# Attention probabilities turned by VectorE blocks and DMA in place of TensorE transposes

## The chip, the cores and the metric

The kernel runs on one core of one Trainium2 chip. A core has a matrix engine (TensorE, PE in the profile), a vector engine (VectorE, DVE), a scalar engine (ScalarE, ACT), a general engine (GpSimd, POOL), a queue engine (SyncE, SP), and sixteen DMA engines that serve the queues of SP, ACT and POOL. PE multiplies a stationary operand, loaded by a separate instruction (PEld in the profile), with a moving one and writes into eight PSUM banks of 128 x 512 float32; DVE and ACT carry results from PSUM to SBUF. [...] Each engine runs its instructions in the order in which they were written out, and waits for other engines and transfers by semaphores.

The metric is the device time of one execution, in microseconds.

## The reference

Two layers over 512 tokens of width 1024 in float32: dilated attention and a gated feed-forward block, then an mLSTM mixer and a second feed-forward block, then a norm. The change touches the attention:

```python
def banded_window_attention(q, k, v, window):
    ...                                     # blocks of 128 queries, each with its own and the previous block of keys
    s = jnp.einsum('...iqd,...ikd->...iqk', qb, kk).astype(jnp.float32)
    s = jnp.where(valid, s, -jnp.inf)
    m = jnp.max(s, axis=-1, keepdims=True)
    p = jnp.exp(s - m)
    den = jnp.sum(p, axis=-1, keepdims=True)
    o = jnp.einsum('...iqk,...ikd->...iqd', (p / den).astype(v.dtype), vv)
    lse = (m + jnp.log(den))[..., 0]
    ...

def dilated_attention_mixer(xn, positions, w_in, w_out):
    proj = (xn @ w_in).reshape(B, S, N_GROUPS, 3, ATTN_HEADS, ATTN_HEAD_DIM)   # 1024 x 9216
    for g, (window, dilation) in enumerate(((128, 1), (512, 4), (2048, 16))):
        q = apply_partial_rope(proj[:, :, g, 0], positions) * scale
        k = apply_partial_rope(proj[:, :, g, 1], positions)
        o, lse = dilated_window_attention(q, k, proj[:, :, g, 2], window, dilation)
        ...
    wts = jax.nn.softmax(jnp.stack(lses), axis=0)
    o = jnp.einsum('gbsh,gbshd->bshd', wts, jnp.stack(outs))
    return o.reshape(B, S, ATTN_WIDTH) @ w_out
```

There are eight heads of 128. Per head the three groups give 15 blocks of 128 queries by 128 keys: seven for group 0 (four diagonal ones and three with the previous block) and four each for groups 1 and 2. The product with the values needs each of these blocks with the keys on the partitions, while the softmax needs them with the queries there: each block of probabilities has to be turned.

## The kernel before

**Projections.** Weights come from DRAM in chunks of 512 KB on SP's queue (`load_chunk`, L186). Each is split into a high and a low part, `_h` by ACT (L198) and `_l` by DVE (L199), with three buffers per part, and each product is three matmuls, high by high, low by high, high by low (`multiply`, L224). `project` (L234) computes 256 columns as two accumulators in two chunks; three PSUM banks (`acc`) hold accumulators. After each chunk it calls `advance()`, which moves a clock of ticks on by one. A tick is 24 matmuls of 512 columns, or 48 of 256 in the token form (`project_tokens`, L251).

**Order around the change.** Attention works on four pairs of heads (`attention_pair`, L451). Per pair there are nine projections, 18 ticks: q and k of groups 0, 1 and 2 (ticks 1 to 12), then v of groups 0, 1 and 2 (13 to 18). The attention work proper is put between the projections' matmuls by `defer(n, fn)`, which calls `fn` n ticks later, and `run` (L155), which keeps the PE instructions of the called functions together as one block: it is issued after the last PE instruction before it, and later projection matmuls are held behind its last one (`fenced`, L167). The places are lists of ticks:

- `scores0` at +2 after k of group 0; the others are counted from the end of the group 2 k projection (tick 12): `scores12` at +3, `weigh` with `turn` at +5, `transposes(0)` at +6, `values(0)` with `transposes(1)` at +7, `values(1)` at +8. The last pair has `LAST_AT`, one tick less from the weigh run on; +7, +8 and so on reach into the projections of the next pair, or, for the last, into the output projection.
- `scores0` (L463) and `scores12` (L486): scores on PE, mask and maximum on DVE, exponentials on ACT, into `p0` (seven blocks) and `p12` (eight blocks) of each head of the pair.
- `weigh` (L539): one PE matmul exchanges sums between token orders (L530), about ten small DVE instructions form the factors, and sixteen DVE instructions scale `p0` and `p12` in place (L560, L563), head 0 first.
- `turn` (L565): turns v of group 0 on PE, from `vf0` in a tag `vf` with one buffer.
- `transposes(i)` (L574): 15 PE transposes of head i's blocks into four PSUM banks (tags `s` and `o`, two each), each carried by ACT to SBUF (L582) into one of `PT_BUFS` = 4 buffers of 128 x 512.
- `values(i)` (L585): 15 matmuls accumulate the head's 128 x 512 output in one PSUM bank (tag `t`, one buffer), which ACT carries out to `o_heads` (L601). In the trace each shows as two records, 14 of line 594 and 16 of line 599.

After the fourth pair, `split_act` splits the finished heads (L213, L214), `last_heads` (L656) the last two; the output projection follows in four column parts of two chunks each, the first inside the attention's scope, with the last pair's late runs in it.

Of the kernel before, what the change touches and what calls it, by code (L numbers as in the profile page):

```python
# [11 lines left out]
F32 = mybir.dt.float32  # L12
# [19 lines left out]
C1 = 6.28125  # L32
C2 = float(np.float32(np.uint32(np.float32(TWO_PI - C1).view(np.uint32) & 0xFFFFF000).view(np.float32)))
C3 = float(np.float32(TWO_PI - C1 - C2))
PT_BUFS = 4
RUN_AT = (2, 3, 5, 6, 7, 8)
LAST_AT = (2, 4, 5, 6, 7)
STACK_AT = (9, 11, 14, 16)
HEAD_AT = ((9, 11, 13), (10, 13, 15), (12, 15, 17), (13, 16, 18), (15, 18, 19), (16, 19, 21), (18, 21, 22), (19, 21, 23))
W_BUFS = 3  # L40
# [30 lines left out]
def tile_hybrid_dilated_attn_mlstm(  # L71
# [8 lines left out]
    def pool(stack, name, **kw):  # L80
        return stack.enter_context(tc.tile_pool(name=name, bufs=1, **kw))
# [50 lines left out]
    def defer(n, fn):  # L132
        later.append((tick[0] + n, next(order), fn))
# [33 lines left out]
    def fenced():  # L167
        return tc.issue_after(fence[0]) if fence[0] is not None else nullcontext()

    def acc_tile(name):  # L170
        return ps.tile([P, 512], F32, tag="acc", name=name, bufs=3)
# [21 lines left out]
    def split_chunk(chunk):  # L193

        raw, n, view, name = chunk
        hi = wp.tile([P, 1024], F32R, tag="whi", name=name + "_h", bufs=W_BUFS)
        lo = wp.tile([P, 1024], F32R, tag="wlo", name=name + "_l", bufs=W_BUFS)
        nc.scalar.activation(hi[:, :n], raw[:, :n], AF.Copy)  # L198
        nc.vector.tensor_tensor(lo[:, :n], raw[:, :n], hi[:, :n].bitcast(F32), op=ALU.subtract)  # L199
        return view(hi), view(lo)  # L200
# [70 lines left out]
    def transpose_into(dst_ps, i, src, n=P):  # L271
        nc.tensor.transpose(dst_ps[:, i * n:(i + 1) * n], src, ident)  # L272
# [38 lines left out]

    with ExitStack() as actx:
        ap = pool(actx, "attn")

        first_w = []
        R = 32
# [32 lines left out]
                nc.gpsimd.tensor_copy(cosn[:, c * P:(c + 1) * P], cs[s])  # L349

        def tok_tile(name):
            return ap.tile([P, 2, SEQ], F32, tag="qk", name=name, bufs=8)


        xt = {}
# [69 lines left out]
        def by_block(t):  # L425

            return t.rearrange("p (c b j) -> p b c j", c=4, b=TB)
# [23 lines left out]
        def attention_pair(pr):  # L451
# [8 lines left out]
            def score_bank(i, name):  # L460
                return ps.tile([P, 512], F32, tag="so"[i], name=name, bufs=2)
# [24 lines left out]
            def scores12(qk1, qk2):  # L486

                for i in range(2):
                    p12[i] = ap.tile([P, 8, P], F32, tag="p12", name="%sp12_%d" % (nm, i), bufs=2)
                    for g, (q, k) in ((1, qk1), (2, qk2)):  # L490
                        sp = score_bank(i, "%ss%d" % (nm, g))
                        for c in range(4):
                            sl = slice(c * P, (c + 1) * P)
                            nc.tensor.matmul(sp[:, sl], q[:, i, sl], k[:, i, sl], start=True, stop=True)
                        for c in range(4):
                            sl = slice(c * P, (c + 1) * P)
                            nc.vector.tensor_tensor_reduce(
                                p12[i][:, 4 * (g - 1) + c, :], sp[:, sl], mask_causal if g == 1 else mask_dil,
                                1.0, -3e38, op0=ALU.add, op1=ALU.max, accum_out=mx[:, g - 1, i, c:c + 1])
                    exponentials(1, i)  # L500
# [71 lines left out]
                                             scale=rnat[:, b:b + 1])  # L572

            def transposes(i):  # L574
                pts[i] = []
                for b, (src, n0, n1) in enumerate(((p0[i], 0, 4), (p0[i], 4, 7), (p12[i], 0, 4), (p12[i], 4, 8))):
                    tp = score_bank(b // 2, nm + "pT")
                    for j in range(n0, n1):
                        transpose_into(tp, j - n0, src[:, j, :])
                    t = ap.tile([P, 512], F32, tag="pt", name=nm + "pTs", bufs=PT_BUFS)  # L580
                    w = (n1 - n0) * P
                    nc.scalar.activation(t[:, :w], tp[:, :w], AF.Copy)  # L582
                    pts[i].append(t)

            def values(i):  # L585
                pt = pts[i]
                hs = slice(i * P, (i + 1) * P)
                op = ps.tile([P, 512], F32, tag="t", name=nm + "o", bufs=1)
                first = True
                for b in range(4):  # L590
                    for kb in range(max(b - 1, 0), b + 1):
                        idx = 2 * b - (b - kb)
                        src = pt[idx // 4][:, (idx % 4) * P:(idx % 4 + 1) * P]
                        nc.tensor.matmul(by_block(op)[:, b], vt[0][:, kb, hs], src,
                                         start=first, stop=False, skip_group_check=True)
                        first = False
                for g in (1, 2):
                    for c in range(4):
                        nc.tensor.matmul(op[:, c * P:(c + 1) * P], vt[g][:, c, hs], pt[1 + g][:, c * P:(c + 1) * P],
                                         start=False, stop=(g == 2 and c == 3), skip_group_check=True)  # L600
                nc.scalar.activation(o_heads[2 * pr + i], op, AF.Copy)  # L601

            qks = []
            for g in range(3):
# [19 lines left out]
                if g == 0:  # L624
                    defer(RUN_AT[0], lambda: run(lambda: scores0(*qks[0])))
            later_runs = (
                (lambda: scores12(*qks[1:]),), (weigh, turn),
                (lambda: transposes(0),), (lambda: values(0), lambda: transposes(1)), (lambda: values(1),))
            for at, fns in zip(RUN_AT[1:] if pr < HEADS // 2 - 1 else LAST_AT, later_runs):
                defer(at, lambda fns=fns: run(*fns))  # L630
            for g in range(3):
                v = ap.tile([P, TB, 256], F32, tag="v", name="%sv%d" % (nm, g), bufs=4)
                vt.append(v)

                def evac_v(m, acc, v=v):
                    for i in range(2):
                        tb = 2 * m + i
                        nc.scalar.activation(v[:, tb, :], acc[:, i * 256:(i + 1) * 256], AF.Copy,
                                             scale=rtok[:, tb:tb + 1])
                if g == 0:  # L640

                    vf0, v0 = ap.tile([P, 2, SEQ], F32, tag="vf", name=nm + "vf"), v

                    def evac_f(m, acc, vf=vf0):
                        nc.scalar.activation(in_order(vf[:, m]), by_block(acc), AF.Copy)
                    project(pair, w_in, 2 * D + pr * 256, KC, evac_f, nm + "g0v")
                else:
                    project_tokens(pair, w_in, g * 3 * D + 2 * D + pr * 256, evac_v, "%sg%dv" % (nm, g))
# [16 lines left out]
        def out_project(pairs, w2d, nk, name, first=0, end=KC // 2):  # L665
            for c in range(first, end):
                project(pairs, w2d, c * 256, nk, add_to_h(c), "%s%d" % (name, c))


        defer(1, last_heads)  # L670
        out_project(pair, attn_w_out[0], KC, "awo", end=1)
        assert not later
    out_project(pair, attn_w_out[0], KC, "awo", first=1)


    def norm(key, k0, name):
# [454 lines left out]
```

## Time and profile before

| | |
|---|---|
| median of the runs | 1482.21 us (1481.99 to 1483.33, three runs) |
| profiled execution | 1481.93 us, span 1479.8 us |
| granted TensorE clock | 0.999 |
| DMA | 134.70 MB, 91 GB/s over the span; SP's queue 28.8% of sixteen engines' time, POOL's 0.1% |
| busy from 30 to 460 us (430 us) | PE 430.00, DVE 246.19, ACT 147.84, POOL 0.00 |

The pairs of attention fill the first 470 us or so. The page shows for each engine how long it was busy. Matmuls overlap, so their lengths add up to more than the time they take; the cost of one is the distance between the starts of two that follow each other. The names in a row are output <- inputs, with buffer numbers left out (`a1pT<-cst,a1p` writes the transposed probabilities of pair 1). The number behind an arrow in a row is the idle time before it and what ended that. A row of DMA issues gives the KB of one transfer and the median time from its issue to its landing.

### The profile page before, as it was taken

The numbers are of one execution on the slowest core, as the hardware profiler recorded it, in microseconds if no ns is written. First come the engines' busy times: TensorE is split into PE (matmuls) and PEld (weight loads), VectorE is DVE, ScalarE is ACT, GpSimd is POOL, SyncE is SP. The second block draws the span as 40 slices with busy tenths as digits, with TensorE's granted clock in tenths as the row PEclk, the third lists the DMA queues.
The fourth block names the chain that finished last, engine by engine and source line by source line (L and its number), as shares of the span: only waits on it lengthen the run. The fifth ranks groups of instructions, "written<-read, shape, count | busy, mean of one in ns | idle before, by whom it ended". The sixth has DMA issues, their size and how long they took to land. (4 is left out here: it accounts for less than half of the span.)

```text
span 1479.8 us, 18900 instructions
## 1 busy us (share of the span) xinstructions
PE 1463.7 (99%) x7484; PEld 1250.0 (84%) x7484; DVE 766.5 (52%) x1507; ACT 545.2 (37%) x997; POOL 102.7 (7%) x94
## 2 busy tenths in 40 slices
PE   7999999999999999999999999999999999999998
PEld 6899889889889888888888889798888888888887
DVE  7754654654665463343343338987755443343233
ACT  5333325225226342232232223785543333233223
POOL 1000000000000001111110000000000111110011
PEclk9999999999999999999999999999999999999999
DMA  6322222232232223333323233231233233322232
GB/s 191 100 86 72 86 86 72 86 96 76 63 99 81 72 87 102 97 100 100 99 84 103 93 94 87 58 100 58 80 106 97 90 98 100 100 92 94 85 100 72
DMA packets 127528, 134.70 MB, mean 91 GB/s; under 512 B 5392, under 2 KB 119376, under 8 KB 127440
## 3 DMA queue, kind: packets, MB, share of 16 engines
q1 hardware_dynamic: 125328, 131.55, 28.8%
q10 hardware_dynamic: 1808, 1.38, 0.3%
q8 instruction: 59, 0.97, 0.3%
q0 software_dynamic: 304, 0.56, 0.1%
q14 instruction: 29, 0.24, 0.0%
HBM read 131.38 MB, written 2.10 MB: 90 GB/s over the span
## 5 line engine op out<-in xcount | busy, mean ns | idle before, releaser
L229 PE MATMUL f0j<-n_h,f0j_h 128*128 128x512 f32 x352 | 137.1, 389 | 0.0
L229 PE MATMUL f1j<-n_h,f1j_h 128*128 128x512 f32 x352 | 137.1, 389 | 0.0
L229 PE MATMUL f0j<-n_h,f0j_l 128*128 128x512 f32 x352 | 137.0, 389 | 0.0
L229 PE MATMUL f1j<-n_h,f1j_l 128*128 128x512 f32 x352 | 137.0, 389 | 0.0
L229 PE MATMUL f0j<-n_l,f0j_h 128*128 128x512 f32 x352 | 136.9, 389 | 0.0
L229 PE MATMUL f1j<-n_l,f1j_h 128*128 128x512 f32 x352 | 136.9, 389 | 0.0
L199 DVE TENSOR_TENSOR f0j_l<-f0j_w,f0j_h 128x1024 fp32r<-128x1024 f32 x44 | 54.8, 1245 | 54.9 <-ACT f0j_h L198 54.8
L199 DVE TENSOR_TENSOR f1j_l<-f1j_w,f1j_h 128x1024 fp32r<-128x1024 f32 x44 | 54.8, 1246 | 54.6 <-ACT f1j_h L198 54.6
L229 PEld LDWEIGHTS f1j<-n_h,f1j_l 128*128 128x128 f32 x352 | 66.1, 188 | 13.9
L229 PEld LDWEIGHTS f0j<-n_h,f0j_l 128*128 128x128 f32 x352 | 66.1, 188 | 13.9
L229 PEld LDWEIGHTS f1j<-n_l,f1j_h 128*128 128x128 f32 x352 | 66.1, 188 | 13.8
L229 PEld LDWEIGHTS f0j<-n_h,f0j_h 128*128 128x128 f32 x352 | 66.1, 188 | 13.8
L229 PEld LDWEIGHTS f0j<-n_l,f0j_h 128*128 128x128 f32 x352 | 66.1, 188 | 13.5
L229 PEld LDWEIGHTS f1j<-n_h,f1j_h 128*128 128x128 f32 x352 | 66.1, 188 | 13.5
L198 ACT ACTIVATE f0j_h<-f0j_w 128x1024 fp32r<-128x1024 f32 x44 | 46.5, 1057 | 73.6 <-PE f0j L229 72.5
L198 ACT ACTIVATE f1j_h<-f1j_w 128x1024 fp32r<-128x1024 f32 x44 | 46.5, 1057 | 73.3 <-PE f1j L229 72.2
L1063 PE MATMUL fin<-fw_h,f1ah 128*128 128x512 f32 (+1 forms) x198 | 72.8, 368 | 0.0
L1063 PE MATMUL fin<-fw_l,f1ah 128*128 128x512 f32 (+1 forms) x198 | 72.5, 366 | 0.0
L1063 PE MATMUL fin<-fw_h,f1al 128*128 128x512 f32 (+1 forms) x198 | 72.4, 366 | 0.0
L229 PE MATMUL fo<-f0ah,fo_k_l 128*128 128x512 f32 x176 | 68.5, 389 | 0.0
L229 PE MATMUL fo<-f0al,fo_k_h 128*128 128x512 f32 x176 | 68.5, 389 | 0.0
L229 PE MATMUL fo<-f0ah,fo_k_h 128*128 128x512 f32 x176 | 68.5, 389 | 0.0
(1160 smaller groups left out, 3569.7 us busy)
## 6 DMA issues: line engine op xcount, KB each, us to landing
f0j_w<-in_ffn_w_in_dram SPq DMA_DIRECT2D x44, 512.0 KB, 3.6
f1j_w<-in_ffn_w_in_dram SPq DMA_DIRECT2D x44, 512.0 KB, 3.5
fw_w<-in_ffn_w_out_dram SPq DMA_DIRECT2D x22, 512.0 KB, 3.8
fo_k_w<-in_ffn_w_out_dram SPq DMA_DIRECT2D x20, 512.0 KB, 3.4
awo_k_w<-in_attn_w_out_dram SPq DMA_DIRECT2D x8, 512.0 KB, 3.5
mv_k_w<-in_mlstm_w_in_dram SPq DMA_DIRECT2D x8, 512.0 KB, 3.7
mqk_k_w<-in_mlstm_w_in_dram SPq DMA_DIRECT2D x8, 512.0 KB, 3.7
mo_k_w<-in_mlstm_w_in_dram SPq DMA_DIRECT2D x8, 512.0 KB, 3.6
```

Of the source, the lines that this page charges most:

```text
L198: nc.scalar.activation(hi[:, :n], raw[:, :n], AF.Copy)
L199: nc.vector.tensor_tensor(lo[:, :n], raw[:, :n], hi[:, :n].bitcast(F32), op=ALU.subtract)
L229: nc.tensor.matmul(acc, whl[a][:, k, m * P:(m + 1) * P], pairs[b][kk], start=(kk == 0 and (a, b) == SPLITS[0]), stop=(kk == nk - 1 and (a, ...
L1063: nc.tensor.matmul(acc[i][:, cs], a[a_][kk][:, tb * P:(tb + 1) * P], whl[b_][:, k, cs], start=(kk == 0 and (a_, b_) == SPLITS[0]), stop=(k ...
```

## The change

The 15 blocks of a head are turned in two steps. DVE's transpose turns each 32 x 32 square of a block in place (one instruction for `p0`, one for `p12`), into a buffer `pB` of 128 x 1920 that shares the one-buffer tag `vf`. Then POOL's DMA queue writes `pB` whole to a scratch tensor in DRAM (`pD`, two buffers), and four more DMAs read it back with the 32-row groups exchanged, each into 32 partitions of `pT` (two buffers). `values` takes its moving operand from `pT` in four pieces of 32 elements.

The runs of a pair go from six to four: `transposes` no longer contains PE work and is called in the weigh run for both heads, and both `values` make one run at +9; in the last pair they are two runs, at +7 and +8. The scores and weigh places stay. The values' accumulator moves to the PSUM tag `o`, which has two buffers. Buffers for q and k go from 8 to 6, for v from 4 to 3. The first two parts of the output projection are written out chunk by chunk for both parts (part 0 chunk 0, part 1 chunk 0, part 0 chunk 1, part 1 chunk 1), the second part's accumulators lie in tag `s`, and `last_heads` is due after two ticks in place of one.

In the order in which the instructions of the changed kernel are written out, DVE has in the weigh run of pairs 0 to 2: the sixteen scalings, the two transposes of head 0, two weight splits of the next projections, the two transposes of head 1 (which wait for head 0's write), then the evictions of the next pair's q. In the last pair, six splits of finished heads and two weight splits lie between the two heads' transposes. POOL has, per head, the write (waiting for DVE), then four reads, the first waiting for the write; head 1's write comes behind head 0's reads.

```diff
-PT_BUFS = 4
-RUN_AT = (2, 3, 5, 6, 7, 8)
-LAST_AT = (2, 4, 5, 6, 7)
+RUN_AT = (2, 3, 5, 9)
+LAST_AT = (2, 4, 7, 8)
...
+        dp = pool(actx, "scratch", space=bass.MemoryType.DRAM)
...
-            return ap.tile([P, 2, SEQ], F32, tag="qk", name=name, bufs=8)
+            return ap.tile([P, 2, SEQ], F32, tag="qk", name=name, bufs=6)
...
             def transposes(i):
-                pts[i] = []
-                for b, (src, n0, n1) in enumerate(((p0[i], 0, 4), (p0[i], 4, 7), (p12[i], 0, 4), (p12[i], 4, 8))):
-                    tp = score_bank(b // 2, nm + "pT")
-                    for j in range(n0, n1):
-                        transpose_into(tp, j - n0, src[:, j, :])
-                    t = ap.tile([P, 512], F32, tag="pt", name=nm + "pTs", bufs=PT_BUFS)
-                    w = (n1 - n0) * P
-                    nc.scalar.activation(t[:, :w], tp[:, :w], AF.Copy)
-                    pts[i].append(t)
+                t = ap.tile([P, 4, 15, R], F32, tag="vf", name=nm + "pB")
+                for src, n0 in ((p0[i], 0), (p12[i], 7)):
+                    n1 = n0 + src.shape[1]
+                    nc.vector.transpose(t[:, :, n0:n1, :].rearrange("p b n i -> p n b i"), src)
+                d = dp.tile([P, 4, 15 * R], F32, tag="d", name=nm + "pD", bufs=2)
+                nc.gpsimd.dma_start(d, t.rearrange("p b n i -> p b (n i)"))
+                pt = pts[i] = ap.tile([P, 4, 15, R], F32, tag="pt", name=nm + "pT", bufs=2)
+                for b in range(4):
+                    nc.gpsimd.dma_start(pt[R * b:R * (b + 1)].rearrange("p a n i -> p a (n i)"),
+                                        d.rearrange("(a j) b x -> b j a x", a=4)[b])
 
             def values(i):
                 pt = pts[i]
                 hs = slice(i * P, (i + 1) * P)
-                op = ps.tile([P, 512], F32, tag="t", name=nm + "o", bufs=1)
+                op = ps.tile([P, 512], F32, tag="o", name=nm + "o", bufs=2)
...
-                        idx = 2 * b - (b - kb)
-                        src = pt[idx // 4][:, (idx % 4) * P:(idx % 4 + 1) * P]
-                        nc.tensor.matmul(by_block(op)[:, b], vt[0][:, kb, hs], src,
+                        nc.tensor.matmul(by_block(op)[:, b], vt[0][:, kb, hs], pt[:, :, 2 * b - (b - kb), :],
                                          start=first, stop=False, skip_group_check=True)
...
-                        nc.tensor.matmul(op[:, c * P:(c + 1) * P], vt[g][:, c, hs], pt[1 + g][:, c * P:(c + 1) * P],
+                        nc.tensor.matmul(op[:, c * P:(c + 1) * P].rearrange("p (a i) -> p a i", a=4),
+                                         vt[g][:, c, hs], pt[:, :, 3 + 4 * g + c, :],
                                          start=False, stop=(g == 2 and c == 3), skip_group_check=True)
...
             later_runs = (
-                (lambda: scores12(*qks[1:]),), (weigh, turn),
-                (lambda: transposes(0),), (lambda: values(0), lambda: transposes(1)), (lambda: values(1),))
+                (lambda: scores12(*qks[1:]),), (weigh, turn, lambda: transposes(0), lambda: transposes(1)))
+            later_runs += (((lambda: values(0), lambda: values(1)),) if pr < HEADS // 2 - 1 else
+                           ((lambda: values(0),), (lambda: values(1),)))
...
-                v = ap.tile([P, TB, 256], F32, tag="v", name="%sv%d" % (nm, g), bufs=4)
+                v = ap.tile([P, TB, 256], F32, tag="v", name="%sv%d" % (nm, g), bufs=3)
...
-        defer(1, last_heads)
-        out_project(pair, attn_w_out[0], KC, "awo", end=1)
+        defer(2, last_heads)
+        acc = [[acc_tile("awo0_%d" % m) for m in range(2)],
+               [ps.tile([P, 512], F32, tag="s", name="awo1_%d" % m, bufs=2) for m in range(2)]]
+        for ch in range(2):
+            for c in range(2):
+                whl = split_chunk(weight_chunk(attn_w_out[0], ch, c * 256, 4, "awo%d_k%d" % (c, ch)))
+                for m in range(2):
+                    with fenced():
+                        multiply(acc[c][m], whl, pair, ch, m, KC)
+                    if ch == 1:
+                        add_to_h(c)(m, acc[c][m])
+                advance()
         assert not later
-    out_project(pair, attn_w_out[0], KC, "awo", first=1)
+    out_project(pair, attn_w_out[0], KC, "awo", first=2)
```

## The prediction

> **What bounds the kernel now.** First the page's table of engines, then who PE waited for, then the timeline of one pair of heads, then the DMA rows nearest to the new transfers.
>
> ```profile
> PE 1463.7 (99%) x7484; PEld 1250.0 (84%) x7484; DVE 766.5 (52%) x1507; ACT 545.2 (37%) x997; POOL 102.7 (7%) x94
> ```
> PE is busy all the time, and in the first 470 us the list of PE's waits has three lines, all in the first 12 us of the kernel:
>
> ```profile
> PE xT L272 <- DMA x_tok<-in_x_dram: 3.9, 1, 3.9
> PE arT L377 <- DMA cst<-in_shape_constants_dram: 2.8, 1, 2.8
> PE xT L272 <- DVE xa_l L217: 1.2, 1, 1.2
> ```
> So in attention the time is the sum of what PE issues: an instruction taken off PE is time won, and any wait put into PE's order is time lost in full. The timeline of pair 1 (start us, length, engine, line):
>
> ```profile
> 232.03 0.39 PE L530 MATMUL a1xps<-a1ex,acst 128*128 128x128 f32 x2
> 233.04 0.36 PE L261 MATMUL a1g2v<-a1g2v_k_h,xa_h 128*128 128x256 f32 x1
> 236.06 1.08 DVE L560 TENSOR_SCALAR a1p<-a1p,a1cf 128x128 f32<-128x128 f32 x4
> 239.09 1.13 DVE L563 TENSOR_SCALAR a1p<-a1p,a1cf 128x256 f32<-128x256 f32 x4
> 238.88 1.80 PE L272 MATMUL a1pT<-cst,a1p 128*128 128x128 f32 x15
> 240.44 0.48 PE L229 MATMUL a2g0q<-xa_h,a2g0q_k_h 128*128 128x512 f32 x1
> 240.75 0.40 PE L229 MATMUL a2g0q<-xa_l,a2g0q_k_h 128*128 128x512 f32 x1
> 245.97 1.72 PE L594 MATMUL a1o<-a1pTs,a1v 128*128 128x128 f32 x14
> 249.32 1.80 PE L272 MATMUL a1pT<-cst,a1p 128*128 128x128 f32 x15
> 242.74 1.22 DVE L199 TENSOR_TENSOR a2g0k_k_l<-a2g0k_k_w,a2g0k_k_h 128x1024 fp32r<-128x1024 f32 x1 [2.52 <-ACT a2g0k_k_h L198]
> ```
> Call the start of the weigh run w (232.03 here). To be seen: the probabilities are scaled by DVE until w+8.2 (239.09 plus 1.13); fifteen transposes hold PE from 238.88 to 240.44; the values of one head hold it from 245.97 to 249.32. A tick of projection on PE is 24 matmuls at a step of 0.227 us (5.45), or 48 at 0.120 in the token form (5.8).
>
> DMA: the only large transfer issued by POOL (512 KB), POOL's queue in half a microsecond of it (packets, MB, share of the 16 engines), weight loads, and the only writes to DRAM:
>
> ```profile
> gbc<-in_final_norm_dram POOLq DMA_DIRECT2D x1, 512.0 KB, 4.7
> q0 software_dynamic: 45, 0.18, 98.4%
> a1g1q_k_w<-in_attn_w_in_dram SPq DMA_DIRECT2D x2, 512.0 KB, 3.5
> out_dram<-ht SPq DMA_DIRECT2D x4, 256.0 KB, 2.0
> x_tok<-in_x_dram SPq DMA_DIRECT2D x4, 512.0 KB, 9.1
> ```
>
> **What goes.** Eight groups of 15 PE transposes, each from 238.88 to 240.44, 1.56 us: 12.5 us. Six runs per pair become four, five in the last; leaving a run costs about 0.1 (240.44 to 240.75 is 0.31 where the step is 0.227), so seven exits give 0.7. Together 13.2 us, all on the path. ACT loses 32 evictions (4 in 1.95 us at 239.81) and DVE gets work instead; neither bounds.
>
> **What comes, and when it must be there.** Values of both heads are now one run at +9 from the fourth tick after weigh: PE goes through the rest of weigh and turn (1.0), one token tick (5.8) and three ticks of the next pair (16.4), so it asks for head 0's block at w+23.2, and after 3.35 us of values for head 1's at w+26.5. That is the deadline. Against it stands one chain, each step waiting for the last:
> - T, DVE's two 32x32 transposes of a head, 896 and 1024 elements per partition. No row shows one. Nearest by length is the one-pass TENSOR_TENSOR over 1024 elements, 1.22 us; I take 1.1 + 1.2 = 2.3. Bounds: 1.4 by the TENSOR_SCALAR rows (0.35 for 256), 4.6 if it needs two passes. All scaling stands ahead of it in DVE's order, so head 0's is done at w+10.5.
> - W, the write of 128 rows of 7,680 B, 0.98 MB. The gbc row: issued at 1070.18, first bytes about 1.7 later, 0.5 MB in 1.4, landed at 4.7, thus 1.6 of tail. At 0.18 MB per 0.5 us, 0.98 MB takes 2.7: 1.7 + 2.7 + 1.6 = 6.0, and 6.1 with the issue. Below: 2.5 for 256 KB (out, ACT's queue) plus 0.72 MB in 2.0, 4.5. Above: 8 or more, as x_tok needs 9.1 for 512 KB when loads queue up.
> - R, four reads that POOL issues after W has landed, 0.25 MB each, at 0.55 us per issue (its rows loads): 1.7 + 2.7 + 1.5, 5.9. Below: a weight load, 3.5, plus 0.46 MB in 1.3, 4.8.
> - T for head 1 writes the same buffer (the tag with one buffer), so it starts only when W of head 0 has landed. DVE blocks there. Two weight splits are ahead of it and end about w+14.7; queued behind it are the evictions of the next pair's q. PE needs the accumulator of the first at w+20.5; with W landing at w+16.6, T ends at w+18.9 and eviction and shuffle at w+20.3. This cover has 0.2 us left, but what it costs when gone is contained in the stall below, not added.
> - W of head 1 waits on POOL behind the four issues of R (2.2 us, as long as T), meets the end of R on the engines: 6.4. Then R.
>
> Sum: w + 10.5 + 6.1 + 2.3 + 6.4 + 5.9 = w+31.2 against w+26.5: PE waits **4.7 us** per pair, in pairs 0 to 2. Head 0's block lands at w+22.5, just in time. Pair 3 weighs one tick earlier and has no split between its small operations (scaling ends at w+7.1), T at w+9.4, block 0 at w+21.4 against w+18.1 (1.0 + 11.6 + 5.45): 3.3; head 1: DVE has six activation splits (2.49 for four) and two weight splits before T, T ends at w+18.9, block at w+31.2 against w+27.0 + 3.3: 0.9. Together 4.2.
>
> A stopped PE may also come back slow. The kernel's first 16 transposes, after a wait of 3.85, take 3.89 us (6.87 to 10.76), where 15 take 1.56 later: up to 2.2 lost, or nothing if that was only the start of the kernel. I take 1.0 per stop, 4.0. [...] The granted clock in the profile's windows stays at 1.00 in that start, so no row of this case settles it.
>
> At nothing: 40 POOL issues (POOL is idle from 16 to 460 us); 15.7 MB more DMA on engines 27% busy there, which may stretch weight loads (issued some 10 us ahead of their split); the reads of the values in pieces of 32 (results in such pieces, L594, cost the same 275 ns as plain ones, L599; if the operand's pieces doubled the step, 27 us); q/k buffers 8 to 6 and v 4 to 3 (the values of a pair end at tick 3 of the next, whose first v is written at tick 17); the values' PSUM bank (its other users come three ticks later). The reordered output projection has the same matmuls, and both heads' splits keep the same cover of some nine matmuls.
>
> **Sum.** The profiled execution took 1481.9 (span 1479.8 and 2.1 around it; the median of the runs is 1482.2). 1481.9 - 13.2 + 3 x 4.7 + 4.2 + 4.0 = **1491 us**, 0.6% slower.
>
> **Rivals.**
> - *In time, faster.* With the low ends (W 4.5, R 4.8) head 1's block lands at w+26.8, block 0 of pair 3 at w+18.8; about 2 us lost in all, 13.2 won: 1470. For it speak the weight and output rows; against it that POOL's one large row took 4.7 for half the bytes. It decides where the waits fall under 3.3 us per pair, that is each leg about 0.5 us shorter than taken and no slow restart. [...] Chance 25%.
> - *Far late.* DVE's transpose needs two passes (4.6): both T's lengthen the chain by 4.6, 3 x 4.6 + 4 more: 1509; legs of 7.5 us give about the same. For it: T's output is written in pieces of 32 elements, which no row of before does on DVE from SBUF, and the four transfers of a pair follow each other within 21 us beside four weight loads. Against it: DVE's shuffle of 512 elements takes 0.72, one pass. Chance 20%, 1506 to 1530.
> - *Even.* Waits near 3.3 and no slow restart cancel the gain: 1479 to 1485, 7%.
>
> **Numbers.** My forecast, waits of 3.5 to 7 us (1485 to 1506), gets 48%. No change means within 0.2%, 3 us, about what a measurement of this kernel can tell. Faster 25%, same 7%, slower 68%. The range 1470 to 1512 takes in the early case and most of the late one.
>
> **What would show it.** PE's list of waits has the values' matmuls waiting for the pT blocks: three pairs with 4 to 5 us on head 1, pair 3 on head 0. DVE has 16 stream transposes of 1.1 and 1.2 us, the third and fourth of each pair waiting for DMA. The write lands in about 6 us, the reads in 4 to 6 each. PE's a1pT group is gone. The prediction is wrong if those PE waits are missing (legs too long in my sum) or sit before the transposes.

## The result, and the profile after

The changed kernel takes **1508.91 us** (median of four runs, 1507.24 to 1510.87) against 1482.11 us: ratio 1.0178, 95% interval 1.0165 to 1.0191, so 1.8% slower. The prediction said 1491. The direction is right and the time lies inside the whole range of 1470 to 1512, but the loss is 26.8 us where 9 was forecast, and it lies above the 1485 to 1506 of the forecast itself, in the band of the rival "far late". The profiled execution took 1508.08 us with a span of 1506.3 us; the mean granted clock fell from 0.999 to 0.990.

The page's table of engines, and behind it PE's list of waits over the first 580 us (engine, what it was about to do, who it waited for: us in total, times, longest):

```profile
PE 1461.3 (97%) x7364; PEld 1246.3 (83%) x7364; DVE 782.8 (52%) x1523; ACT 530.7 (35%) x965; POOL 124.6 (8%) x134
```

```profile
PE a2o L595 <- DMA a2pT<-a2pD: 8.0, 2, 6.0
PE a0o L595 <- DMA a0pT<-a0pD: 7.6, 2, 6.5
PE a1o L595 <- DMA a1pT<-a1pD: 7.6, 2, 6.7
PE a3o L595 <- DMA a3pT<-a3pD: 5.7, 1, 5.7
PE xT L271 <- DMA x_tok<-in_x_dram: 5.1, 2, 4.0
PE arT L377 <- DMA cst<-in_shape_constants_dram: 2.8, 1, 2.8
```

PE issues 120 instructions fewer, the transposes. In exchange there are four new waits, all on the read back, 28.9 us in sum. Where the time was lost follows from the starts of the weigh runs and of `n1bc` (the norm behind the output projection):

```profile
116.19 0.39 PE L530 MATMUL a0xps<-a0ex,acst 128*128 128x128 f32 x2
240.01 0.39 PE L530 MATMUL a1xps<-a1ex,acst 128*128 128x128 f32 x2
363.37 0.39 PE L530 MATMUL a2xps<-a2ex,acst 128*128 128x128 f32 x2
482.56 0.39 PE L530 MATMUL a3xps<-a3ex,acst 128*128 128x128 f32 x2
570.44 0.62 PE L295 MATMUL n1bc<-n1dg,ones_r 128*128 128x512 f32 x2
```

Before, these five stand at 115.06, 232.03, 348.99, 460.21 and 543.75. The stretches between them grow by 6.9 (pair 0), 6.4 (pair 1), 8.0 (pair 2) and 4.3 us (pair 3 with the output projection); the start adds 1.1; behind `n1bc` the two kernels take the same time (936.1 before, 935.9 now). But for that start, everything was lost inside the four pairs.

Pair 1 from its weigh run at w = 240.01 (start, length, engine, line; the idle time before a row and what ended it in brackets), with the new chain of transposes (T), write (W) and reads (R):

```profile
248.12 2.23 DVE L580 STREAM_TRANSPOSE a1pB<-a1p 128x896 f32<-128x896 f32 x2
255.68 2.24 DVE L580 STREAM_TRANSPOSE a1pB<-a1p 128x896 f32<-128x896 f32 x2 [1.01 <-DMA a1pD<-a1pB]
250.64 0.56 POOL L582 DMA_DIRECT2D a1pD<-a1pB  x1 [105.28 <-DVE a1pB L580]
256.16 2.18 POOL L585 DMA_DIRECT2D a1pT<-a1pD  x4 [4.96 <-DMA a1pD<-a1pB]
258.33 0.56 POOL L582 DMA_DIRECT2D a1pD<-a1pB  x1
266.74 2.18 POOL L585 DMA_DIRECT2D a1pT<-a1pD  x4 [7.85 <-issue]
264.24 1.80 PE L595 MATMUL a1o<-a1pT,a1v 128*128 128x128 f32 x14 [0.87 <-DMA a1pT<-a1pD]
274.54 3.36 PE L595 MATMUL a1o<-a1pT,a1v 128*128 128x128 f32 x14 [6.71 <-DMA a1pT<-a1pD]
277.69 2.04 PE L600 MATMUL a1o<-a1pT,a1v 128*128 128x128 f32 x16
279.48 0.48 PE L228 MATMUL a2g0k<-xa_h,a2g0k_k_h 128*128 128x512 f32 x1
```

Each leg is the distance from an issue to what it releases. Head 0: the write from 250.64 to 256.16, 5.5 us; the reads from 256.16 to 264.24, 8.1. Head 1: the write from 258.33 to 266.74, 8.4; the reads from 266.74 to 274.54, 7.8. The values of head 1 then last from 274.54 to 279.48, 4.9 us in place of 3.35.

That last row is the second loss. The windows of pair 0, in which PE stands still from about 144.3 to 150.8 (busy us of PE, PEld, DVE, ACT, POOL; then granted clock, DMA share, GB/s):

```profile
146.00:148.00 2.00, 0.00 (x0) 0.00 (x0) 0.00 (x0) 0.00 (x0) 0.00 (x0) 1.00 1.05 237
148.00:150.00 2.00, 0.00 (x0) 0.00 (x0) 0.00 (x0) 0.00 (x0) 0.00 (x0) 0.54 0.66 130
150.00:152.00 2.00, 1.21 (x6) 1.24 (x7) 0.00 (x0) 0.00 (x0) 0.00 (x0) 0.50 0.00 0
152.00:154.00 2.00, 2.00 (x11) 2.00 (x11) 0.00 (x0) 0.00 (x0) 0.00 (x0) 0.50 0.00 0
154.00:156.00 2.00, 2.00 (x16) 2.00 (x16) 0.00 (x0) 0.00 (x0) 0.00 (x0) 0.75 0.00 0
156.00:158.00 2.00, 2.00 (x12) 1.71 (x11) 0.00 (x0) 0.60 (x1) 0.00 (x0) 1.00 0.00 0
```

The granted clock falls to 0.50 in the course of the stop, and PE works at about half speed for some time after it has its data: in pair 1 the first fourteen matmuls of head 1's values take 3.36 us, those of head 0 1.80. In pair 0 the clock fell 3.8 us into the stop (144.3 to about 148.2) and came back 4.2 us behind the restart (150.8 to about 155). In the windows of pairs 1, 2 and 3 it fell 3.2, 5.1 and 2.4 us into the stop and came back 3.3, 5.9 and 3.5 us behind the restart, so neither time is fixed; it stood at 0.50 for 6.8 us in each of the four pairs.

### The profile page after: what moved, and what is told of

Read it like the earlier page. It is cut to its first block, busy times and chain, and to the rows that moved or that the text cites. A ratio compares the mean times of both kernels' runs of the same rounds, so it can differ in the third digit from the quotient of the medians.

```text
span 1506.3 us, 18718 instructions
## 1 busy us (share of the span) xinstructions
PE 1461.3 (97%) x7364; PEld 1246.3 (83%) x7364; DVE 782.8 (52%) x1523; ACT 530.7 (35%) x965; POOL 124.6 (8%) x134
```

## The experiments

The working theory A: the loss is PE's waits for the read back and the cold restarts behind them, and nothing else. Its rivals: the new traffic or the buffer counts cost something by themselves (B, C), or a later place only moves the wait. A second question was why the legs are longer than forecast. All kernels were compared with the kernel before on the same chip in the same sitting.

**Nothing waits.**

```diff
-    ..., vt[0][:, kb, hs], pt[:, :, 2 * b - (b - kb), :], ...
+    ..., vt[0][:, kb, hs], p0[i][:, 2 * b - (b - kb), :], ...
-    nc.tensor.matmul(op[...].rearrange("p (a i) -> p a i", a=4), vt[g][:, c, hs], pt[:, :, 3 + 4 * g + c, :], ...
+    nc.tensor.matmul(op[...], vt[g][:, c, hs], p12[i][:, 4 * (g - 1) + c, :], ...
```

> What it leaves out: the value products read the weighted probabilities as they stand (p0, p12), unturned, so the attention output is another than the reference's; the block turns, both DMA legs, the runs' places and the count of matmuls stay. TensorE so waits for nothing of the chain, while VectorE and the DMA queue carry the whole new load. Theory A (the loss is TensorE's waits for the read back, 28.9 us in the changed kernel's profile, and the four cold restarts of about 2 us each behind them): 1508.9 - 28.9 - 8 = 1472, anything from 1467 to 1475, ten microseconds faster than the kernel before, and no stretch at a granted clock of 0.50 around the value products. Theory B (the new traffic also holds up weight loads, evictions or VectorE's other work): 1480 or more, with waits on weights or on VectorE's results that the kernel before does not have.

Measured: 1469.24 us (1468.52 to 1469.89), ratio 0.9909 (0.9894 to 0.9923). Theory A holds. With all 15.7 MB of new DMA traffic and all of DVE's transposes still there, the kernel is 12.8 us faster than before, which is the gain that the prediction had worked out (13.2). The traffic, the forty issues on POOL, the smaller buffers and the other PSUM bank cost PE nothing to be seen. The difference to the changed kernel, 39.7 us, is 28.9 of waits and 10.8 of the rest, in which the start of the profiled executions has 0.6 (pair 0's weigh run begins at 115.63 here); it leaves about 2.5 per pair for what a stop costs beyond its own length.

**Two places later.**

```diff
-RUN_AT = (2, 3, 5, 9)
+RUN_AT = (2, 3, 5, 11)
```

> The value products of pairs 0 to 2 run two places later (place 11 in place of 9, some 13 us: TensorE then asks for head 0's block about 36 us behind the start of the weigh run and for head 1's about 39 us behind it, and the slowest block landed 34.5 us behind it). The last pair is left alone. Theory A: the waits of pairs 0 to 2 (7.6, 7.6 and 8.0 us) and about 2 us of cold restart each go, so 1508.9 - 23.2 - 6 = 1480, between 1476 and 1484; the last pair still waits 5.7 us. Theory B (the wait only moves, as the value products now meet the next pair's scores in the PSUM banks and in VectorE's queue): 1490 or more.

Measured: 1477.23 us (1476.29 to 1477.45), ratio 0.9961 (0.9947 to 0.9976). Of the waits on the read back one is left:

```profile
PE a3o L595 <- DMA a3pT<-a3pD: 5.6, 1, 5.6
```

From one weigh run to the next, pairs 0 and 1 take 113.70 us each here (116.21, 229.91 and 343.61), to the hundredth what they take in the run that waits for nothing (115.63, 229.33 and 343.03), and 116.97 before. The same chain, no shorter, costs nothing in three of the four pairs once there is other work in front of PE. One number turns the loss into a small gain.

**TensorE's transposes put back, the rest of the change kept.** `transposes`, the six runs and `PT_BUFS` of the kernel before; the smaller query, key and value buffers and the reordered output projection of the changed one. The values' accumulator stands in bank `t` here, as in the kernel before, and not in `o` as the expectation has it.

```diff
-RUN_AT = (2, 3, 5, 9)
-LAST_AT = (2, 4, 7, 8)
+PT_BUFS = 4
+RUN_AT = (2, 3, 5, 6, 7, 8)
+LAST_AT = (2, 4, 5, 6, 7)
...
```

> TensorE's transposes, their evictions and the six runs per pair (five in the last) are put back; everything else of the change stays (six query/key buffers for eight, three value buffers for four, the output accumulator in bank o, the output projection with its first chunks for two column groups ahead). Theory A (the whole loss is the turn through DRAM and its waits): 1482, within 2 us of the kernel before. Rival C (the smaller buffer counts or the reordered output projection carry part of the loss, say the 4.3 us that the last pair and the output projection lost): 1485 to 1500.

Measured: 1482.22 us (1481.72 to 1484.18), ratio 1.0000 (0.9990 to 1.0009). Rival C is out: the smaller buffers and the reordered output projection cost nothing. For the bank, the traffic and the issues the run without waits stands.

**Both writes ahead of the reads.** Head 1's turned blocks get their own space, so T of head 1 waits for nobody, and POOL issues W, W, R, R.

```diff
-                t = ap.tile([P, 4, 15, R], F32, tag="vf", name=nm + "pB")
+                t = ap.tile([P, 4, 15, R], F32, tag="vf" if i == 0 else "qk", name=nm + "pB", **({} if i == 0 else {"bufs": 3}))
...
-(weigh, turn, lambda: transposes(0), lambda: transposes(1)))
+(weigh, turn, lambda: transposes(0), lambda: transposes(1), lambda: read_back(0), lambda: read_back(1)))
```

> Head 1's turned blocks get a buffer of their own (in the slots of the query and key tiles, now three double ones), and GpSimd issues both writes before the first read, so that head 1's write no longer stands behind head 0's reads. Theory D (the chain is long because its four legs run one behind the other, each paying its own start): both writes landed by about 18.5 us behind the weigh run's start, head 0's reads by 24.5, head 1's by 29, so the waits shrink from 7.6 to 2.5 or 3.5 per pair: 1485 to 1494. Rival E (the DMA engines' bytes are the limit, reads at 0.23 MB per us and writes at 0.42 taking turns): head 0's block comes later as its read shares the engines with the second write, head 1's hardly earlier than 33 us, and the time stays between 1502 and 1510.

Measured: 1493.64 us (1490.17 to 1494.21), ratio 1.0068 (1.0053 to 1.0083): at the upper edge of what theory D expected. The waits, 3.6 to 5.5 us in pairs 0 to 2, are longer than its 2.5 to 3.5. POOL's rows of pair 0, then PE's waits behind the start of the kernel:

```profile
125.85 0.58 POOL L584 DMA_DIRECT2D a0pD<-a0pB  x1 [109.86 <-DVE a0pB L582]
127.97 0.54 POOL L584 DMA_DIRECT2D a0pD<-a0pB  x1 [1.55 <-DVE a0pB L582]
130.22 2.23 POOL L591 DMA_DIRECT2D a0pT<-a0pD  x4 [1.71 <-DMA a0pD<-a0pB]
134.32 2.18 POOL L591 DMA_DIRECT2D a0pT<-a0pD  x4 [1.88 <-DMA a0pD<-a0pB]
```

```profile
PE a2o L601 <- DMA a2pT<-a2pD: 5.5, 2, 3.5
PE a1o L601 <- DMA a1pT<-a1pD: 5.1, 2, 3.4
PE a0o L601 <- DMA a0pT<-a0pD: 3.6, 1, 3.6
PE awo L228 <- DVE awo_k_l L198: 2.5, 1, 2.5
```

Two writes are through in 8.5 us (125.85 to 134.32), where one behind the other took 5.5 and 8.4 with the reads' issues between. But part of rival E is true as well: head 0's block lands only at 142.22, some 12 us behind its read's issue (8.1 in the changed kernel). That the second write and then the second read share the engines with it is the likely reason; what the chain saved in starts and what in bytes was not separated. The fourth wait is new: the output projection waits for a weight split.

**Why a read is slower than a write.** In the changed kernel a microsecond of a write and one of a read, by the DMA queues of 1 us windows (packets, MB, share of the 16 engines), are:

```profile
q0 software_dynamic: 58, 0.45, 112.7%
q0 software_dynamic: 62, 0.24, 107.1%
```

In these two microseconds the way back moves at half the rate, with the engines full both times. The read differs from the write in its direction, in its 1920-byte pieces, and in filling 32 partitions per transfer. Two kernels change the partitions or the pieces alone, a third both; reads they stay, so a fast one speaks against the direction as well. All three leave out the exchange of the blocks.

```diff
-                for b in range(4):
-                    nc.gpsimd.dma_start(pt[R * b:R * (b + 1)].rearrange("p a n i -> p (a n i)"),
-                                        d.rearrange("(a j) b x -> b j a x", a=4)[b])
+                nc.gpsimd.dma_start(pt.rearrange("p a n i -> p (a n i)"), d.rearrange("p b x -> p (b x)"))   # r128_7680
...
+                for a in range(4):                                                                           # r128_1920
+                    nc.gpsimd.dma_start(pt[:, a].rearrange("p n i -> p (n i)"), d[:, a])
...
+                for b in range(4):                                                                           # r32_7680
+                    nc.gpsimd.dma_start(pt[R * b:R * (b + 1)].rearrange("p a n i -> p (a n i)"),
+                                        d[R * b:R * (b + 1)].rearrange("p b x -> p (b x)"))
```

> Only the read back is changed: one DMA per head fills all 128 partitions with each row of the scratch as it lies there, 7680 bytes in one piece (what it leaves out: the exchange of the blocks, so the attention output is another than the reference's). In the changed kernel the reads moved 0.20 to 0.24 MB per us with the DMA engines full, the writes 0.37 to 0.45. Theory P (a read that fills only 32 partitions at a time is slow) and theory S (a read in pieces of 1920 bytes is slow) both expect a read as fast as the write: leg R 5.4 in place of 7.6 to 8.5 us, the second write no longer 8.4 but 6.2, so head 1's block 7 us earlier, the two waits of a pair together about 1 in place of 7.6, and 1508.9 - 4 x 7 = 1481, between 1476 and 1488. Theory Q (reading this scratch back is slow in itself, whatever its shape): no gain but the three issues saved, 1504 to 1509.

> Again only the read back: four DMAs per head as in the changed kernel, with the same 1920-byte pieces in the scratch, but each fills a quarter of the free axis of all 128 partitions in place of the whole of 32 (the blocks stay unexchanged, so the attention output is another). Theory P: as fast as the write, 0.37 MB per us or more, 1478 to 1490. Theory S: as slow as before or slower (1920-byte pieces on both sides), 0.24 MB per us or less, 1504 to 1512. Theory Q: 1504 to 1509.

> The fourth corner: four DMAs per head, each filling 32 partitions, but with whole rows of 7680 bytes (the blocks stay unexchanged, so the attention output is another). Theory P: as slow as the changed kernel, 0.20 to 0.24 MB per us, 1504 to 1510. Theory S: as fast as the write, 1478 to 1488. Theory Q: 1504 to 1509.

| read of a head | time, us | ratio (95%) |
|---|---|---|
| 4 x 32 partitions, pieces of 1920 (the changed kernel) | 1508.91 | 1.0178 (1.0165 to 1.0191) |
| 4 x 32 partitions, rows of 7680 | 1508.67 | 1.0172 (1.0157 to 1.0187) |
| 4 x 128 partitions, pieces of 1920 | 1499.91 | 1.0118 (1.0101 to 1.0135) |
| 1 x 128 partitions, rows of 7680 | 1499.87 | 1.0115 (1.0100 to 1.0130) |

Windows of 1 us differ much, so here is the queue over the whole of head 1's read in pair 0, in the order of the table (windows 143.5 to 151, 143.5 to 151.6, 141.2 to 148.5 and 144.5 to 150):

```profile
q0 software_dynamic: 256, 0.98, 60.9%
q0 software_dynamic: 192, 0.98, 53.5%
q0 software_dynamic: 256, 0.98, 38.5%
q0 software_dynamic: 144, 0.98, 49.8%
```

The share times the length of the window is the time that the 0.98 MB would take with all engines full: 4.6 and 4.3 us with 32 partitions, 2.8 and 2.7 with 128. Piece size does not make this difference, and neither does the direction (the write of head 0 in pair 1 of the changed kernel, over 128 partitions, comes to 3.2: 73.2% of 250.6 to 255); the partitions do. The factor is 1.5 to 1.7, and 1.4 for head 0's read in pair 1 (4.5 against 3.3 with one read into 128).

In time the runs with 128 partitions gained 9 us where theory P expected some 28, so they lie outside the ranges of all three theories, and the transfer rate is not the whole of a leg. Pair 1 with one read into 128 partitions:

```profile
254.74 0.53 POOL L584 DMA_DIRECT2D a1pT<-a1pD  x1 [4.85 <-DMA a1pD<-a1pB]
256.84 0.54 POOL L582 DMA_DIRECT2D a1pD<-a1pB  x1 [1.57 <-DVE a1pB L580]
263.04 1.83 PE L593 MATMUL a1o<-a1pT,a1v 128*128 128x128 f32 x14 [0.97 <-DMA a1pT<-a1pD]
266.13 0.53 POOL L584 DMA_DIRECT2D a1pT<-a1pD  x1 [8.76 <-DMA a1pD<-a1pB]
271.19 3.36 PE L593 MATMUL a1o<-a1pT,a1v 128*128 128x128 f32 x14 [4.54 <-DMA a1pT<-a1pD]
```

Only head 1's read became shorter, 5.1 us in place of 7.8. Head 0's still took 8.3 (254.74 to 263.04), and head 1's write even 9.3 (256.84 to 266.13) in place of 8.4. In the changed kernel weight loads fill the engines when head 0's read is issued; SP's queue (255 to 258) shows

```profile
q1 hardware_dynamic: 964, 0.97, 100.5%
```

and the read's first bytes come at about 258. With one read into 128 partitions the engines are full as well behind the issue of head 0's read in pair 0 at 133.21 (97% from 133 to 134, 107% from 134 to 135). What else holds up these two legs with the faster read is not shown. PE still waits 5.5 to 7.1 us per pair there in pairs 0 to 2.

**The exchange moved to the write.**

```diff
-                nc.gpsimd.dma_start(d, t.rearrange("p b n i -> p b (n i)"))
+                for a in range(4):
+                    nc.gpsimd.dma_start(d.rearrange("(b j) a x -> a j b x", b=4)[a],
+                                        t[R * a:R * (a + 1)].rearrange("p b n i -> p b (n i)"))
...
+                nc.gpsimd.dma_start(pt.rearrange("p a n i -> p (a n i)"), d)
```

> The block exchange is moved from the read to the write: four writes per head, each from 32 partitions of the turned tile into the scratch in its final order, in 1920-byte pieces, and one read per head of whole rows into 128 partitions. The output is the same as the changed kernel's. Theory P, if a write from 32 partitions is as slow as a read into 32 (0.23 MB per us, about 8 us a write), and the read takes the 6.8 us of the run with one read into 128 partitions: head 0's block some 1.5 us later, head 1's some 1 us earlier or later, so 1505 to 1512. Theory P', only a read into 32 partitions is slow and a write from 32 is not: the time of the run with one read into 128 partitions, 1498 to 1502.

Measured: 1522.03 us (1520.98 to 1522.31), ratio 1.0261 (1.0247 to 1.0275): slower than either expectation. The write of 32 partitions at a time is slow too (first row, one window with nothing else on the engines: 0.20 MB per full microsecond; 4.4 us of full engines over the whole write, 54.7% of 127 to 135), and the expectation had missed VectorE's order (its rows behind, pair 0):

```profile
q0 software_dynamic: 32, 0.18, 89.4%
```

```profile
137.98 1.28 DVE L445 TENSOR_TENSOR a1g_q<-a1g_q,rot 32x512 f32<-32x512 f32 x2
139.19 2.22 DVE L580 STREAM_TRANSPOSE a0pB<-a0p 128x896 f32<-128x896 f32 x2
```

The write took 8.5 us from issue to release and was through at 135.54, but head 1's transposes stood in the written order behind the evictions and the rotation of the next pair's q and came at 139.19. In the changed kernel they stand ahead of these and came at 131.98. Write and pieces were changed together here, so this run alone does not say which of the two slows the write.

**Is it the halves of the partitions?** Head 1's read over 32 partitions kept the engines full 1.7 times as long as the one over 128 (4.6 to 2.7, above). The guess tested here, which no run above shows: if the limit belonged to each half of the partitions, two reads into different halves would run side by side.

```diff
-                for b in range(4):
+                for b in (0, 2, 1, 3):                                             # order
...
-                    nc.gpsimd.dma_start(pt[R * b:R * (b + 1)].rearrange("p a n i -> p (a n i)"),
+                    (nc.gpsimd if b < 2 else nc.sync).dma_start(pt[R * b:...       # two queues
```

> Only the order of the four reads of a head is changed: partition groups 0, 2, 1, 3 in place of 0, 1, 2, 3, all from GpSimd's queue as before; the output is the changed kernel's. Theory P1 (the half rate belongs to each half of the partitions, 0 to 63 and 64 to 127, and two reads into different halves can run at the full rate side by side): neighbours in the queue now lie in different halves and overlap, so a part of the 9 us that reads into all 128 partitions gained: 1500 to 1505, and over 0.28 MB per us with the engines full. Theory P2 (a transfer of 32 partitions runs at half rate whatever stands beside it, or the queue works its transfers off one by one): 1507 to 1510, and 0.20 to 0.24 MB per us.

> The reads into partition groups 0 and 1 stay on GpSimd's queue, those into 2 and 3 go to SyncE's, between its weight loads (for head 0 behind the load that follows next, where SyncE then waits for the write); the output is the changed kernel's. Theory P1: the two halves fill at once, the read leg falls from 7.6 or 8.5 to 5.5 or 6, GpSimd is also free two issues earlier, and the waits of a pair fall from 7.6 to about 2: 1482 to 1495. Theory P2: each read still moves at 0.20 to 0.24 MB per us in sum: 1503 to 1510. Rival (SyncE's wait for the write holds up the weight loads behind it, and TensorE waits for weights in place of the blocks): 1500 or more with waits on the weight splits.

Measured: 1505.31 us (1505.06 to 1508.03), ratio 1.0161 (1.0144 to 1.0178) for the order, and 1507.41 us (1504.78 to 1508.60), 1.0167 (1.0152 to 1.0182) for the two queues. Both intervals overlap that of the changed kernel. The first lies between the two theories, the second where P2 has it; PE's waits on the read back came to 25.0 and 26.0 us in place of 28.9, and none on weight splits appeared. Windows of 1 us of head 1's read in pair 0, for the order (one line) and for the two queues (both queues of one window):

```profile
q0 software_dynamic: 82, 0.30, 94.7%
```

```profile
q0 software_dynamic: 37, 0.14, 50.6%
q1 hardware_dynamic: 71, 0.13, 50.1%
```

That is a little more than 0.22 per full microsecond (0.32 and 0.27). Over the whole read the order comes to 3.6 us of full engines (48.2% of 142.6 to 150) in place of 4.6, against 2.7 with all 128 partitions. The halves side by side gave a part of that in engine time, and hardly any of it in the kernel's time. SyncE's queue moved its reads in packets of some 1.8 KB (0.13 MB in 71), GpSimd's in 3.8 KB, which weakens the second comparison. So "a transfer over 32 partitions keeps the DMA engines busy 1.4 to 1.7 times as long" is shown, and what inside is full is not settled.

**All in one.** Places 11, then a third column group of the output projection ahead of the last two heads (`e8_best`), then with the two writes ahead of the reads as well (`e10_both`).

```diff
-RUN_AT = (2, 3, 5, 9)
-LAST_AT = (2, 4, 7, 8)
+RUN_AT = (2, 3, 5, 11)
+LAST_AT = (2, 4, 8, 9)
...
+               [acc_tile("awo2_0"), ps.tile([P, 512], F32, tag="t", name="awo2_1", bufs=1)]]
...
-            for c in range(2):
+            for c in range(3):
```

> All of the change with later value products: place 11 in pairs 0 to 2, and in the last pair places 8 and 9 with the first four chunks of a third column group of the output projection moved ahead of the last heads' products, so that these are asked for about 6.5 us later than in the changed kernel, against a wait of 5.7 there. Theory A (waits and cold restarts are the whole loss): the run with place 11 alone, 1477.2, less 5.6 of wait and 2 of restart: 1469.5, between 1467.5 and 1472. Rival (the third column group needs an accumulator in bank t and the last accumulation bank, and TensorE waits for these in place of the read back): 1474 to 1480.

Measured: 1475.50 us (1472.45 to 1476.10), ratio 0.9945 (0.9930 to 0.9960), 6 us more than theory A had it. The wait of head 0 is gone, and head 1's took its place:

```profile
475.37 1.78 PE L595 MATMUL a3o<-a3pT,a3v 128*128 128x128 f32 x14
487.82 3.33 PE L595 MATMUL a3o<-a3pT,a3v 128*128 128x128 f32 x14 [3.41 <-DMA a3pT<-a3pD]
```

The expectation had looked only at the wait in the list. In the changed kernel head 1 of the last pair did not wait because head 0's stop had delayed PE. Take the first wait away and the second block is the late one: it landed at 487.8.

> The overlap of the two writes (a buffer of its own for head 1's turned blocks, both writes issued ahead of the reads), the value products at place 11 in pairs 0 to 2, and the last pair's at 8 and 9 with the third column group ahead. Theory A: no wait for the read back is left, in the last pair neither (head 1's block landed 3.4 us late in the run without the overlap, and the overlap brought it some 4 us forward), so the time of the run whose value products waited for nothing, 1469.2, within 2 us. Rival (the third column group or the smaller buffers cost what they free): 1472 to 1477, with waits of the output projection's matmuls on its weights or accumulators.

Measured: **1471.97 us** (1471.67 to 1472.66), ratio 0.9925 (0.9912 to 0.9939): the fastest full version, 11 us faster than the kernel before beside it (1483.30) and 37 faster than the changed one. No wait for the read back is left. It is 2.7 us above the run without waits, between theory A and its rival; the two intervals (0.9912 to 0.9939, 0.9894 to 0.9923) overlap. In the profiled executions, 3.6 apart, pair 0's weigh run begins at 117.55 here and at 115.63 there, 1.9 of it, and the output projection waits once for its weights, as the rival expected:

```profile
PE awo L228 <- DVE awo_k_l L198: 1.5, 1, 1.5
```

The third column group is not its cause: the run with only the writes ahead has such a wait too (2.5), and `e8_best` has none. Whether the order of the transfers or the buffers that go with it make it was not separated.

## Why the prediction was right or wrong

**What goes: right.** 13.2 us were forecast; without waits the kernel is 12.8 us faster.

**When the blocks are asked for: right.** Head 0's at w+23.2 forecast, w+23.4 measured (264.24 less 0.87). Head 1's request then follows behind head 0's 0.9 us stop, at w+27.8.

**T: right.** 2.3 us forecast, 2.23 measured (the lower bound of 1.4 was a slip: 0.35 us for 256 elements is 1.4 for 1024 and 2.6 for a head's 1920); one pass, so the main ground of the rival "far late" did not come about.

**W of head 0: a little too long.** 6.1 forecast, 5.5 measured. The row of another transfer from POOL was a fair stand-in for a write of 128 partitions.

**R: the step that failed.** 5.9 us per head were forecast, with 2.7 of them on the engines, by the rate of the same row (0.18 MB in half a microsecond). Measured were 8.1 and 7.8 (pair 1), with 4.5 on the engines. The row was not of the reads' shape: four transfers of 32 partitions move 0.22 MB per full microsecond where the row has 0.36, as the four read shapes show. For head 1's read this is the whole account, since over 128 partitions its leg takes 5.1. For head 0's it is not, since that leg stays at 8.3 with the faster read; there the cause stays open in part.

**W of head 1: mis-sized with it.** 6.4 forecast, 8.4 measured. It was allowed to meet "the end of R"; but its issue stands at 258.33, right behind the four issues of R, and its queue moves at the reads' rate until 263, so it met the whole of R. A faster R alone did not cure that (9.3 us over 128 partitions). Putting both writes ahead of the reads did: issued behind W of head 0, it took 6.4 (127.97 to 134.32), and the kernel some 15 us less.

Together: T of head 1 ended early (w+17.9 against w+18.9) and its write was issued 0.6 us ahead of the forecast; W and R then took 2.0 and 1.9 more. Head 1's block came at w+34.5 in place of w+31.2. PE's waits became 28.9 in place of 18.3, 10.6 us of the 17.9 by which the prediction missed.

**The slow restart: mis-sized too.** 1.0 per stop, 4.0 in all, was the middle between nothing and 2.2. Pair by pair, growth plus gain less wait leaves 2.5 (6.9 + 3.3 - 7.6), 2.1, 3.3 and 1.8 us, 9.7 in sum. The prediction said that no row settled it and took the middle; the four remainders lie around its upper end, 2.2, and the granted clock stood at 0.50 behind each stop. PE worked at 0.50 for 4.2, 3.3, 5.9 and 3.5 us behind the four restarts; half of that, 2.1, 1.7, 2.9 and 1.7, is an estimate of what the clock cost. It goes with the four remainders pair by pair and leaves 1.3 of the 9.7. Beyond the 4.0 forecast, the 9.7 are 5.7 us of the miss. Another 1.1 is the start of the kernel: pair 0's weigh run begins between 114.9 and 117.6 in the profiles of kernels that do the same work up to there. Half a microsecond is left over; the median lies 0.8 above the profiled execution that these rows are from.

**The rivals.** "In time" failed on the legs: its low ends were 4.5 and 4.8 us, and in pair 1 they were 5.5 to 8.4. "Far late" named the size that came, legs of about 7.5 us and 1509, with a chance of 20%, and its argument that four transfers of a pair follow each other beside weight loads was the one that held; its main ground, two passes of T, was not. "Even" did not come. What was put at nothing cost PE nothing in the changed kernel.

## What to carry to other kernels

A duration borrowed from another transfer did not hold here for another shape on the on-chip side: the bytes over 32 partitions took 4.3 to 4.6 us of full engines and the same bytes over 128 took 2.7 to 3.3, in pieces of either size. And a leg is more than its bytes: of the 8.1 us of head 0's read they took 4.5, and the rest went to its start, its landing and the weight loads ahead of it on the engines. When a chain through DMA replaces work on the bounding engine, first ask where its consumer stands in the order, for in pairs 0 to 2 the same chain made PE wait 23.2 us in all at place 9 and not at all at place 11; and list every block's landing time against its request, since the first wait hides the second. The stops of 5.7 to 6.7 us cost TensorE their own length and 1.8 to 3.3 us behind them.

## What the runs showed of the hardware

- A transfer over 32 partitions moved some 0.22 MB per microsecond of full engines (0.98 MB in 4.3 to 4.6 us; 0.20 in a window of the write), a read into 128 partitions 0.30 to 0.36 over its whole length, a write from 128 partitions 0.30 and 0.41 (head 0's, pairs 1 and 3). Two queues filling different halves of the partitions at once came to 0.27 in sum, in a window of 1 us.
- In each pair of the changed kernel the granted clock stood at 0.50 for 6.8 us; it fell 2.4 to 5.1 us into the stop and came back 3.3 to 5.9 us behind the restart. The stops of 0.9 to 1.9 us in front of head 0's values in pairs 0 to 2 left it at 1.00.
- 0.98 MB per head and leg of extra DMA traffic (15.7 MB in all, DMA engines 40% busy from 120 to 460 us in the fastest version) did not make PE wait for a single weight of the pairs; the output projection waited once, 1.5 us.
- DVE transposed 128 x 896 and 128 x 1024 float32 in 32 x 32 squares in 2.23 us together, 1.10 and 1.20 each, where its plain operation over 1024 (a weight split) took 1.22.
- Values read in pieces of 32 elements took the same 1.72 us for 14 matmuls (place 11, pair 1) as values read in one piece (the kernel before, pair 1).
